# Low parts of weight tiles: from a subtraction on GpSimd to a negating copy on ScalarE and an accumulating DMA, with VectorE behind the LayerNorm

## The chip, the cores and the metric

The kernel runs on one core of a Trainium2 chip. The metric is the device time of one execution in microseconds (us); lower is better. Engines are TensorE (PE in the profile, PEld for its weight loads), VectorE (DVE), ScalarE (ACT), GpSimd (POOL) and SyncE (SP), which issues DMAs.

## The reference, cut to what matters

Two layers of a backbone are computed for 128 context tokens and 512 latent tokens, width 1024, all in float32. Each layer normalizes and modulates its input, applies one combined input projection and four branches (A convolution with LayerNorm, B long "Hyena" convolution, C pooling, D attention), gates and projects each branch, merges them and applies an output projection.

```python
def parallel_mixer(h, p, latent, k_ctx, v_ctx):
    u = h @ p['w_in']                                  # 1024 x 11264
    ...
    ya = (conformer_conv(a_glu, ...) * silu(a_gate)) @ p['wo_conv']
    yb = (hyena(b_proj, ...) * silu(b_gate)) @ p['wo_hyena']
    yc = (multiscale_pool(c_in, ...) * silu(c_gate)) @ p['wo_pool']
    yd = (att * silu(d_gate)) @ p['wo_attn']
    gm = sigmoid(g_merge).reshape(B, L, N_BRANCH, D_MODEL)
    merged = gm[:, :, 0] * ya + gm[:, :, 1] * yb + gm[:, :, 2] * yc + gm[:, :, 3] * yd
    return merged @ p['w_out'], k, v
```

## The kernel before, in words

All 640 tokens go through a layer together. A product of a weight matrix and an activation keeps float32 accuracy by splitting both into a high part (the type fp32r, which TensorE multiplies in one pass) and a low part (the remainder): each block of 128 rows costs three matmuls, high by high, high by low and low by high (`proj`, line 378). A matmul's weights are a tile of 128 partitions by up to 1024 columns: eight blocks of 128x128 for a slice of the input projection, four for the projections of the branches with 512 channels, one for the pooling matrices.

`weights` (line 331) makes such a tile. It takes a place in the ring `wr` (three places, `NHI`), SyncE loads the float32 weights into a buffer `raw` (two buffers, `NRAW`; line 340), ScalarE casts them into `whi` (line 341), and the low part `wlo` is `raw - whi`, written by GpSimd or VectorE (line 342). The flag `pooled[0]` chooses: it is false for the first three tiles of the program and during the output projection of each layer (`out_proj`, line 1758), and true otherwise. A `raw` buffer is free for its next load once `wlo` is written; `whi` and `wlo` are free once TensorE has read them.

The order of work: per layer `layers` runs the Hyena inputs, gates, values, keys and first queries; the Hyena convolutions, attention and their helpers are threads beside it. Then follow the merge of branch B, the inputs of convolution and pooling, the merge of attention (`merge`, line 796: for each of eight blocks one tile of `w_in` for the gate and one of the branch's projection), the pooling gate (`Pooling.gated`: four pairs of a `w_in` tile and a 128x128 pooling matrix), the merge of pooling, the convolution's gate, its merge and the output projection. `Conv.norm` is a thread: the LayerNorm of branch A, which ends (line 1636) while the merge of pooling runs.

TensorE's order is written out by a planner (`Loom`): it keeps a clock per engine from rough costs, runs the thread that could start first by priority, and counts the work of `weights` as background that only advances the clock of its engine. The other engines' orders are set by a scheduler from priorities, with `weights` moved ahead by `WAHEAD` (120). Every engine runs its own list in order, and SyncE's DMAs wait in order too. Instructions of VectorE, ScalarE and GpSimd carry the line of a helper, 179, matmuls 194, transposes 203.

Of the kernel before, what the change touches and what calls it, by code (L numbers as in the profile page):

```python
# [12 lines left out]
AF = mybir.ActivationFunctionType  # L13
ALU = mybir.AluOpType
# [52 lines left out]
def r32(ap):  # L67
    return ap.bitcast(F32)
# [165 lines left out]
def hybrid_flow_backbone(ctx: ExitStack, tc: tile.TileContext, i, o):  # L234
    nc = tc.nc
    lm = Loom()
    pe = Tensor(lm, nc.tensor)
    dve = Engine(lm, nc.vector, "dve", 1.0, 75)
    act = Engine(lm, nc.scalar, "act", 0.84, 130)
    pool = Engine(lm, nc.gpsimd, "pool", 2.1, 150)  # L240
# [19 lines left out]
    def nm(p):  # L260
        count[0] += 1
        return f"{p}{count[0]}"
# [65 lines left out]
        lm.dma = max(lm.dma, lm.issue + 1.2) + int(np.prod(dst.shape)) * 4 / 360e3  # L328
        return lm.dma + 1.9

    def weights(src, kk, n, pl=False):
        yield from wr.get()
        lm.bg = True
        with tc.high_priority(offset=WAHEAD):
            raw = wp.tile([P, 1024], F32, tag="raw", name=nm("raw"), bufs=NRAW)
            hi = wp.tile([P, 1024], F32R, tag="whi", name=nm("whi"), bufs=NHI)
            lo = wp.tile([P, 1024], F32R, tag="wlo", name=nm("wlo"), bufs=NHI)
            w = kk * n
            rv = raw[:, 0:w]
            sp.dma_start(out=rv.rearrange("p (k c) -> p k c", k=kk), in_=src)  # L340
            act.copy(hi[:, 0:w], rv)
            (pool if pooled[0] or pl else dve).tensor_tensor(out=lo[:, 0:w], in0=rv, in1=r32(hi[:, 0:w]), op=ALU.subtract)
        lm.bg = False
        return (hi[:, 0:w].rearrange("p (k c) -> p k c", k=kk),
                lo[:, 0:w].rearrange("p (k c) -> p k c", k=kk))

    def w_cols(l, c0):
        return weights(i["w_in"][l][:, c0:c0 + 128].rearrange("(k p) c -> p k c", p=P), 8, 128)
# [447 lines left out]
    def merge(l, b, ga, nk, wo, merged, mode, ma=None, wait=None):  # L796


        for d in range(8):
            th = yield from tr.get(T)  # L800

            def gate(j, ps):
                act.activation(out=th[:, 320 * j:320 * j + 320], in_=ps, func=AF.Tanh, scale=0.5)

            yield from in_proj(l, C_GM + b * D + 128 * d, gate)
            if wait is not None:
                yield wait
            w = yield from weights(wo[:, 128 * d:128 * d + 128].rearrange("(k p) c -> p k c", p=P), nk, 128)
            def take(j, ps):
                tj = th[:, 320 * j:320 * j + 320]  # L810
                dve.scalar_tensor_tensor(out=tj, in0=tj, scalar=1.0, in1=ps, op0=ALU.add, op1=ALU.mult)

            yield from both(w, 0, ga, nk, take)
            wr.put(WD)
            if mode == "first":
                sp.dma_start(out=mscr[l, d], in_=th)
                lm.cur.t += 2.5
            else:
                yield lambda: 0.0 if len(merged) == 2 else INF
                mv = merged[d // 4].v((d % 4) * T, T)  # L820
                dve.tensor_tensor(out=mv, in0=mv, in1=th, op=ALU.add)
                if mode == "last":
                    split(ma.h(d), ma.l(d), mv, 0.5)
            tr.put()

    hT = [None]
    pooled = [False]
# [691 lines left out]
    class Conv:  # L1519
# [58 lines left out]
        def norm(self):  # L1578
# [55 lines left out]
            sc.put()  # L1634
            co.free()
            self.ev_norm.set()

        def gated(self):
            l = self.l
# [425 lines left out]
```

## Time and profile before

| what | value |
|---|---|
| median of 3 runs (lowest, highest) | 2356.2 us (2354.53, 2362.07) |
| the profiled execution: its own time, its span | 2361.16 us, 2359.4 us |
| mean granted clock of TensorE | 0.977 |
| busy: TensorE, VectorE, ScalarE, GpSimd | 94%, 66%, 41%, 32% of the span |
| DMA, mean over the span | 80 GB/s |

The profile is of one execution, 5.0 us above the median of the runs. A stage is a stretch of the span: the first layer's Hyena stage lies at 60 to 340 us, its attention at 340 to 790, its dense projections up to 1190; the second layer has them at 1240 to 1560, 1560 to 1900 and up to the end. In a row of the trace the text `out<-in` gives tiles: `whi`, `wlo`, `raw` are the weights, `mm`, `ax`, `sc` are banks of PSUM, `sl`, `t`, `u`, `k`, `wx`, `nb` are work tiles in SBUF.

### The profile page before, as it was taken

The numbers are of one execution on the slowest core, as the hardware profiler recorded it, in microseconds if no ns is written. First come the engines' busy times: TensorE is split into PE (matmuls) and PEld (weight loads), VectorE is DVE, ScalarE is ACT, GpSimd is POOL, SyncE is SP. The second block draws the span as 40 slices with busy tenths as digits, with TensorE's granted clock in tenths as the row PEclk, the third lists the DMA queues.
The fourth block names the chain that finished last, engine by engine and source line by source line (L and its number), as shares of the span: only waits on it lengthen the run. The fifth ranks groups of instructions, "written<-read, shape, count | busy, mean of one in ns | idle before, by whom it ended". The sixth has DMA issues, their size and how long they took to land.

```text
span 2359.4 us, 39530 instructions
## 1 busy us (share of the span) xinstructions
PE 2216.7 (94%) x15951; PEld 2161.7 (92%) x15951; DVE 1558.2 (66%) x2962; ACT 960.2 (41%) x1900; POOL 747.1 (32%) x423
## 2 busy tenths in 40 slices
PE   5999989999999999999979888899999999999999
PEld 3988878999999999999969888899989999999999
DVE  4887897577558997133477787956675599842343
ACT  4533335555554224222354332455556532332231
POOL 1745432112222333333056353221212233333320
PEclk8999999999999999999989998999999999999999
DMA  8333321112112322233532211111111132222332
GB/s 266 103 106 95 107 74 54 60 57 62 46 45 77 98 62 83 77 94 90 167 120 57 58 48 45 48 58 61 57 51 49 43 115 72 59 86 72 99 98 85
DMA packets 284804, 189.10 MB, mean 80 GB/s; under 512 B 8445, under 2 KB 275901, under 8 KB 284366
## 3 DMA queue, kind: packets, MB, share of 16 engines
q1 hardware_dynamic: 284622, 186.59, 26.1%
q8 instruction: 125, 2.05, 0.4%
q14 instruction: 57, 0.47, 0.1%
HBM read 174.34 MB, written 12.22 MB: 79 GB/s over the span
## 4 chain that ended last, share of the span: by engine, by line
PE 56%; DVE 17%; ACT 2%; issue 1%; POOL 1%; DMA 0%; ACTq 0%; POOLq 0%; DVEq 0%; SPq 0%
PE mm L194 46%; DVE sl L179 6%; PE sc L194 4%; PE ax L194 3%; PE ax L203 3%; DVE u L179 2%; DVE sc L179 2%; DVE nb L179 1%; DVE k L179 1%; DVE wx L179 1%; DVE h L179 1%; ACT u L179 1%; DVE t L179 1%; DVE rt L179 1%; POOL sl L179 1%
## 5 line engine op out<-in xcount | busy, mean ns | idle before, releaser
L194 PE MATMUL mm<-sl,whi 128*128 128x320 f32 x6304 | 1420.2, 313 | 7.8 <-DVE t L179 5.0
L194 PEld LDWEIGHTS mm<-sl,whi 128*128 128x128 f32 x6304 | 1054.9, 189 | 15.5 <-DVE t L179 4.0
L194 PE MATMUL mm<-sl,wlo 128*128 128x320 f32 x3152 | 979.9, 311 | 0.9 <-DVE wlo L179 0.9
L179 POOL TENSOR_TENSOR wlo<-raw,whi 128x1024 fp32r<-128x1024 f32 (+2 forms) x253 | 550.0, 2174 | 1209.5 <-ACT whi L179 1122.9
L194 PEld LDWEIGHTS mm<-sl,wlo 128*128 128x128 f32 x3152 | 596.0, 189 | 1.2 <-DVE wlo L179 1.2
L179 ACT CAST whi<-raw 128x1024 fp32r<-128x1024 f32 (+2 forms) x272 | 255.3, 939 | 521.6 <-PE mm L194 371.3
L194 PE MATMUL mm<-whi,sl 128*128 128x256 f32 x1600 | 295.0, 286 | 0.3 <-ACT t L179 0.3
L179 DVE SCALAR_TENSOR_TENSOR t<-t,mm 128x320 f32<-128x320 f32 x192 | 92.8, 484 | 269.0 <-PE mm L194 212.2
L194 PE MATMUL sc<-sl,sl 128*128 128x128 f32 (+1 forms) x1344 | 219.3, 309 | 48.7 <-DVE sl L179 26.1
L194 PEld LDWEIGHTS mm<-whi,sl 128*128 128x128 f32 x1600 | 248.2, 190 | 2.3 <-issue 1.2
L194 PEld LDWEIGHTS sc<-sl,sl 128*128 128x128 f32 x1344 | 190.2, 206 | 55.7 <-issue 25.5
L194 PE MATMUL mm<-wlo,sl 128*128 128x256 f32 x800 | 226.0, 282 | 0.0
L179 DVE SCALAR_TENSOR_TENSOR sc<-sl,prm,sc 128x640 f32<-128x640 f32 (+14 forms) x232 | 207.0, 892 | 7.4 <-ACT sc L179 2.5
L179 DVE TENSOR_TENSOR h<-ax,h 128x512 fp32r<-128x512 f32 (+1 forms) x200 | 117.4, 602 | 137.9 <-ACT h L179 137.4
L179 ACT ACTIVATE u<-sc,nb,rq 128x640 f32<-128x640 f32 x128 | 113.4, 886 | 111.4 <-DVE nb L179 88.8
L194 PEld LDWEIGHTS mm<-wlo,sl 128*128 128x128 f32 x800 | 152.3, 190 | 0.2 <-POOL wlo L179 0.2
L179 ACT ACTIVATE t<-mm 128x320 f32<-128x320 f32 x208 | 90.1, 434 | 144.1 <-PE mm L194 143.6
L203 PE MATMUL ax<-ident,u 128*128 128x128 f32 x752 | 117.2, 277 | 15.2 <-DVE sl L179 12.0
L179 ACT CAST h<-ax 128x512 fp32r<-128x512 f32 (+1 forms) x200 | 99.9, 519 | 71.8 <-PE ax L203 70.5
L194 PE MATMUL ax<-h,sl 128*128 128x256 f32 (+1 forms) x656 | 120.0, 295 | 1.2 <-DVE h L179 0.8
L179 DVE TENSOR_REDUCE nb<-sc 128x1 f32<-128x640 f32 x128 | 104.9, 819 | 19.7 <-PE sc L194 19.0
L203 PEld LDWEIGHTS ax<-ident,u 128*128 128x128 f32 x752 | 93.1, 142 | 21.7 <-issue 12.4
(193 smaller groups left out, 2246.7 us busy)
## 6 DMA issues: line engine op xcount, KB each, us to landing
raw<-in_w_in_dram SPq DMA_DIRECT2D x176, 512.0 KB
wlo<-in_w_ada_dram SPq DMA_DIRECT2D x19, 512.0 KB
whi<-in_w_ada_dram SPq DMA_DIRECT2D x19, 512.0 KB
raw<-in_wo_attn_dram SPq DMA_DIRECT2D x16, 512.0 KB
raw<-in_w_out_dram SPq DMA_DIRECT2D x16, 512.0 KB
sl<-in_c_decay_dram SPq DMA_DIRECT2D x16, 320.0 KB
mscr<-t SPq DMA_DIRECT2D x16, 320.0 KB
sl<-mscr SPq DMA_DIRECT2D x4, 1280.0 KB
```

The costliest lines, as they stand in the source:

```text
L179: r = f(*args, **kw)
L194: r = self.real.matmul(out, lhsT, rhs, **kw)
L203: r = self.real.transpose(out, in_, ident)
```

## The change

Where `pooled[0]` is true, the low part is now made in two steps: ScalarE writes `-whi` into `wlo`, and a DMA issued by GpSimd adds `raw` to it. Where it is false, VectorE subtracts, as before. `pooled[0]` is set to false at the end of `Conv.norm` in each layer (it is set to true again as before). The unused argument `pl` goes. GpSimd's other work stays.

```diff
-    def weights(src, kk, n, pl=False):
+    def weights(src, kk, n):
...
             act.copy(hi[:, 0:w], rv)
-            (pool if pooled[0] or pl else dve).tensor_tensor(out=lo[:, 0:w], in0=rv, in1=r32(hi[:, 0:w]), op=ALU.subtract)
+            if pooled[0]:
+
+                act.activation(out=lo[:, 0:w], in_=r32(hi[:, 0:w]), func=AF.Copy, scale=-1.0)
+                nc.gpsimd.dma_start(out=r32(lo[:, 0:w]), in_=rv, accum_op=ALU.add)
+            else:
+                dve.tensor_tensor(out=lo[:, 0:w], in0=rv, in1=r32(hi[:, 0:w]), op=ALU.subtract)
...
             sc.put()
             co.free()
             self.ev_norm.set()
+            pooled[0] = False
```

Over the program, 253 subtractions on GpSimd become 187 pairs of a copy on ScalarE and a DMA on GpSimd's queue (157 of 1024 columns, 22 of 512, 8 of 128), and 66 more subtractions on VectorE (32 of 1024 columns, 34 of 512), which had 19. The engines' orders move at these places. Names: a number stands for one buffer's use, and differs between the two programs.

GpSimd's list in the second layer's Hyena convolutions, before (`sl` of 640 and `wx` of 128 columns are products and sums of the spectra):

```order
L179 TENSOR_TENSOR sl_14152<-sl_12677,sl_13773 128x640
L179 TENSOR_TENSOR wx_12037<-sl_12677 128x128 x2
L179 TENSOR_TENSOR wlo_14896<-raw_14894,whi_14895 128x1024
L179 TENSOR_TENSOR sl_13780<-sl_12677,sl_12824 128x640
L179 TENSOR_TENSOR wx_12037<-sl_12677 128x128 x2
L179 TENSOR_TENSOR wlo_15040<-raw_15038,whi_15039 128x1024
```

and the same place after the change:

```order
L179 TENSOR_TENSOR sl_14256<-sl_12740,sl_13874 128x640
L345 DMA wlo_14937<-raw_14935 128x1024
L179 TENSOR_TENSOR wx_12129<-sl_12740 128x128 x2
L179 TENSOR_TENSOR sl_13881<-sl_12740,sl_12936 128x640
L345 DMA wlo_15007<-raw_15005 128x1024
L179 TENSOR_TENSOR wx_12129<-sl_12740 128x128 x2
```

The DMA takes the subtraction's place in the list, one product earlier or later.

ScalarE's list in the first layer's pooling gate after the change, from the cast of one `w_in` tile to the copy of the next (`sl<-t` is the high part of a gated pooling output, `t<-mm` a gate):

```order
L179 CAST whi_9511<-raw_9510 128x1024
L179 CAST sl_9412<-sl_7636 128x512
L179 ACTIVATE wlo_9512<-whi_9511 128x1024
L179 CAST sl_9412<-sl_7636 128x128
L179 CAST sl_9412<-sl_7636 128x512
L179 ACTIVATE t_9416<-mm_9424 128x320
L179 CAST whi_9576<-raw_9575 128x128
L179 ACTIVATE t_9416<-mm_9457 128x320
L179 ACTIVATE wlo_9577<-whi_9576 128x128
L179 CAST whi_9596<-raw_9595 128x1024
L179 ACTIVATE sl_9412<-t_9416 128x640
L179 ACTIVATE wlo_9597<-whi_9596 128x1024
```

The rows `wlo<-whi` are new; the last of them stands behind a copy that waits for VectorE.

VectorE's list in the merge of pooling, behind the LayerNorm, after the change:

```order
L179 TENSOR_TENSOR wlo_10425<-raw_10423,whi_10424 128x1024
L179 TENSOR_TENSOR wlo_10483<-raw_10481,whi_10482 128x512
L179 SCALAR_TENSOR_TENSOR t_10328<-t_10328,mm_10393 128x320
L179 SCALAR_TENSOR_TENSOR t_10328<-t_10328,mm_10407 128x320
L179 TENSOR_TENSOR sl_8374<-sl_8374,t_10328 128x640
```

The two subtractions are new; the other three rows, which gate one block and add it to the merged sum, followed each other directly before.

## Rows read from the trace of the kernel before

**Rows 1.** The page's busy time, share of the span and instructions, by engine.

```profile
PE 2216.7 (94%) x15951; PEld 2161.7 (92%) x15951; DVE 1558.2 (66%) x2962; ACT 960.2 (41%) x1900; POOL 747.1 (32%) x423
```

**Rows 2.** Windows by stage: length, busy us per engine (instructions), clock, DMA share, GB/s.

```profile
60.00:340.00 280.00, 258.32 (x2012) 245.78 (x2013) 233.13 (x415) 110.38 (x218) 142.11 (x93) 0.98 0.33 100
340.00:790.00 450.00, 427.28 (x3080) 418.66 (x3080) 313.54 (x727) 235.75 (x498) 99.28 (x45) 0.99 0.20 60
1240.00:1560.00 320.00, 280.74 (x2014) 277.37 (x2014) 257.06 (x520) 119.81 (x243) 130.14 (x81) 0.92 0.17 51
1560.00:1900.00 340.00, 329.71 (x2397) 323.62 (x2396) 209.28 (x487) 189.68 (x399) 71.06 (x32) 0.99 0.19 57
```

**Rows 3.** Groups by form: GpSimd, 1240 to 1560 us; ScalarE, whole run: busy us, mean ns.

```profile
L179 POOL TENSOR_TENSOR wlo<-raw,whi 128x1024 fp32r<-128x1024 f32 x25 | 64.3, 2573 | 69.2 <-ACT whi L179 69.2
...
L179 ACT CAST whi<-raw 128x1024 fp32r<-128x1024 f32 x208 | 218.2, 1049 | 377.8 <-PE mm L194 234.5 <-issue 118.7 <-PE ax L194 9.5
```

**Rows 4.** Groups by form on VectorE, 1240 to 1560 us: busy us, mean ns.

```profile
L179 DVE TENSOR_TENSOR sl<-wx 128x512 f32<-128x512 f32 x44 | 45.3, 1067 | 1.0
L179 DVE SCALAR_TENSOR_TENSOR sl<-t,prm,sl 128x641 f32<-128x641 f32 x24 | 33.7, 1408 | 12.3 <-ACT sl L179 12.1
L179 DVE TENSOR_TENSOR wx<-sl,sl 128x640 f32<-128x640 f32 x8 | 11.4, 1425 | 0.2
```

**Rows 5.** The tile wx on VectorE, whole run: duration ns min/median/max.

```profile
L179 DVE TENSOR_TENSOR sl<-wx x96: 674/684/2900, 64.2 to 1478.4; 128x512 f32<-128x512 f32 x96
L179 DVE TENSOR_TENSOR sl<-sl,wx x16: 810/812/819, 119.0 to 1472.7; 128x640 f32<-128x640 f32 x16
```

**Rows 6.** Chain of waits, 1240 to 1560 us: shares by engine, tile and line.

```profile
by line: DVE sl L179 25.5%; PE mm L194 19.3%; PE sc L194 13.0%; DVE wx L179 8.1%; PE ax L194 4.3%; DVE k L179 4.3%; POOL sl L179 4.1%; issue 3.5%; DVE rt L179 3.0%; PE ax L203 2.3%; POOL wlo L179 1.5%; DVE kv L179 1.3%; DVE qv L179 1.1%; DV
```

**Rows 7.** The tile nb on VectorE: whole run (min/median/max); 340 to 790 us (mean).

```profile
L179 DVE TENSOR_TENSOR nb<-nb,rq x128: 142/158/1941, 369.6 to 1883.0; 128x1 f32<-128x1 f32 x128
...
L179 DVE TENSOR_TENSOR nb<-nb,rq 128x1 f32<-128x1 f32 x64 | 20.0, 313 | 1.2
```

**Rows 8.** Waits of TensorE, whole run: us in total, times, longest.

```profile
PE sc L194 <- ACT u L179: 11.9, 11, 2.1
```

**Rows 9.** The page's DMA queues: packets, MB, share of 16 engines.

```profile
q1 hardware_dynamic: 284622, 186.59, 26.1%
```

**Rows 10.** Timeline, steady part of attention's output projection: start us, us, instruction.

```profile
823.77 0.37 SPq L340 DMA_DIRECT2D raw<-in_wo_attn_dram  x1
...
837.69 0.37 SPq L340 DMA_DIRECT2D raw<-in_wo_attn_dram  x1
...
835.26 2.40 POOL L179 TENSOR_TENSOR wlo<-raw,whi 128x1024 fp32r<-128x1024 f32 x1 [4.67 <-ACT whi L179]
...
848.38 0.31 PE L194 MATMUL mm<-sl,wlo 128*128 128x320 f32 x1
```

**Rows 11.** Timeline, pooling gate of the first layer, by engine.

```profile
887.19 0.37 SPq L340 DMA_DIRECT2D raw<-in_w_in_dram  x1
...
894.91 0.37 SPq L340 DMA_DIRECT2D raw<-in_w_in_dram  x1
...
903.29 0.37 SPq L340 DMA_DIRECT2D raw<-in_w_in_dram  x1
...
912.33 0.37 SPq L340 DMA_DIRECT2D raw<-in_w_in_dram  x1
...
922.68 0.37 SPq L340 DMA_DIRECT2D raw<-in_w_in_dram  x1
...
891.36 1.05 ACT L179 CAST whi<-raw 128x1024 fp32r<-128x1024 f32 x1 [0.35 <-PE mm L194]
...
892.49 2.40 POOL L179 TENSOR_TENSOR wlo<-raw,whi 128x1024 fp32r<-128x1024 f32 x1 [1.28 <-ACT whi L179]
...
901.02 0.31 PE L194 MATMUL mm<-sl,wlo 128*128 128x320 f32 x1
```

**Rows 12.** Groups by form on VectorE, 945 to 1190 us.

```profile
L179 DVE TENSOR_TENSOR wlo<-raw,whi 128x1024 fp32r<-128x1024 f32 x8 | 9.8, 1222 | 21.3 <-ACT whi L179 21.2
```

## The prediction

> **What bounds the kernel now.** Read the busy line first: TensorE is busy 94% of the span, so an edit on other engines can win only the time in which TensorE stands still, and can lose whatever it makes TensorE wait for [rows 1]. The table by stage says where it stands still: 21.7 us in the first layer's Hyena stage (280.00 less 258.32), 22.7 us in its attention, 39.3 us in the second layer's Hyena stage, 10.3 us in its attention [rows 2]. In the stage from 1240 us the granted clock is also 0.92, so part of that stretch ran at 1.2 instead of 2.4 GHz. Outside these four stages TensorE loses little but the start and the change of layer.
>
> The chain of waits in the second Hyena stage says who is late there: VectorE's rows add up to 43.3% of it (25.5, 8.1, 4.3, 3.0, 1.3 and 1.1), GpSimd's subtractions of weights to 1.5% [rows 6]. VectorE is slow there because GpSimd works beside it. An addition of 128x512 from two SBUF operands takes 684 ns in the median of its 96 cases, but 2900 at worst, and 1067 in the mean of this stage; a two-operand pass over 640 columns takes 812 ns where nothing disturbs it [rows 5], while the 641-column short convolution takes 1408 and the spectrum product 1425 here [rows 4]. GpSimd's subtraction for a full weight tile is 2573 ns long there, 25 times [rows 3].
>
> The dense stages (attention's output, pooling, convolution and output projections) are the opposite: TensorE never waits, and the question is how far ahead the weights are. In the steady part loads into one raw buffer go out at 823.77 and 837.69, 13.9 us apart for two tiles, the second as soon as GpSimd is done with that buffer at 835.26 + 2.40 = 837.66; TensorE reads that low part at 848.38, so it is 10.7 us ahead [rows 10]. In the pooling gate, where each pair of tiles is one of 7 us and one of under 1 us of TensorE, the lead has shrunk to 901.02 − (892.49 + 2.40) = 6.1 us, and loads go out 7.72, 8.38, 9.04 and 10.35 us apart [rows 11].
>
> **The change part by part.** *Removed:* 253 subtractions on GpSimd, the full ones some 2.5 us each [rows 3]. *Added:* 187 negating copies on ScalarE (157 of 1024 columns, 22 of 512, 8 of 128) and 187 accumulating DMAs, issued by GpSimd, from the raw tile into the low tile. *Moved:* 66 subtractions to VectorE, 32 full and 34 half, all behind the LayerNorm.
>
> The 66 on VectorE cost 1.22 us a full tile [rows 12], about 32 × 1.22 + 34 × 0.7 = 63 us, in stages where TensorE is saturated and they end sooner than GpSimd's 2.5 us would. VectorE's idle time hides them; I count them as 0. If that cover were gone, the lead of the weights on TensorE would have to be used up first.
>
> *ScalarE.* A copy of 1024 columns takes 1.05 us [rows 3], so 157 + 11 + 1 full ones are 177 us more on an engine that has 960 [rows 1], 18%. TensorE waits for ScalarE's exponentials 11.9 us in all [rows 8]; 18% of that is 2 us, and for its other users I take 4 us in total (bounds 0 and 15, by every wait for an exponential more than doubled).
>
> *Relief of VectorE.* In the second Hyena stage three groups lose 44 × (1067 − 684) = 16.9, 24 × (1408 − 812) = 14.3 and 8 × (1425 − 812) = 4.9 us, 36 us together [rows 4, 5]. Weight tiles are about half of GpSimd's work there (64.3 of 130.14 us [rows 2, 3]), and 43% of the chain is VectorE's. From below that is 36 × 0.5 × 0.43 = 8 us; from above it is the whole pause, 39 us. I take 20, since GpSimd's own queue shortens too. For the first layer's Hyena stage I take 10 of its 21.7 us, by the same half. In attention the small product nb on the chain of scores takes 313 ns in the mean where its median is 158: 64 × 155 ns = 9.9 us in one layer [rows 7]; I take 7 for both layers. Gains: 37 us; from below 8, from above the four pauses, 94.
>
> *The price of the DMA.* No row shows an accumulating DMA. Call X the time from the end of the negating copy to the low part being usable and the raw buffer being free. A load of 512 KB takes at most 891.36 − 887.19 = 4.17 us from issue to use [rows 11]. The queue moved 186.59 MB in 26.1% of sixteen engines' span [rows 9], or 303 KB per us, so 524 KB are 1.73 us of it and 2.44 us are fixed. Bounds for X: 2.4 us if only the fixed part counts, 10 if issuing by software doubles it and three passes (read, read, write) follow each other. One pass gives 4.2, two passes 5.9. I take 5.0, between them, because rows here are 4 KB in SBUF instead of the 512-byte pieces of a weight column block.
>
> The Trainium skill (DMA: Bandwidth & Descriptors, Anatomy of one DMA) puts a DMA issued by GpSimd at 2.0 us plus its bytes at 436 GB/s, and the page Collectives: The Full Stack (on ReduceScatter) gives an adding transfer half the rate because of its second read. Estimated from these two, X is 2.0 + 2.4 = 4.4 us and the sum below would be 7 us better; no run so far shows either.
>
> *What X costs.* In the dense stages the raw buffers set the pace, since there are two: load, cast, negate, accumulate, load again. That takes 4.17 + 1.05 + 0.1 + 1.05 + X = 6.4 + X, and at X = 5 it is 11.4 us. In the steady part two full tiles come every 13.9 us, so nothing is lost, and the lead of 10.7 us falls by X + 1.05 − 2.4 = 3.65 to about 7. In the pooling gate 11.4 stands against 7.72, 8.38, 9.04 and 10.35: short by 3.7, 3.0, 2.35 and 1.05, with the first 3.65 makes 13.7, less the lead of 6.1: some 8 us of waiting per layer, 16 in all. As a rule for two layers: 2 × (5X − 17.4) us, nothing below X = 3.5. SP's queue holds its later loads back behind each raw load that waits; in the second Hyena stage 25 tiles come in 320 us, 12.8 us apart, so nothing hangs on that at this X.
>
> *Sum against the profiled execution, 2361.2 us:* −20 − 10 − 7 + 4 + 16 = −17, so 2344. The median of the runs shown lies 5.0 us below that execution; the forecast is 2339 us.
>
> **The rivals.** *The accumulation is slow and the weights become the bound.* If X is 8 us, the cycle is 14.4 us; the pooling gate is short by 6.7 + 6.0 + 5.4 + 4.05 + 6.65 − 6.1 = 23 us, with the pair behind it about 28 per layer, 56 in all, less 33 of net gain: +23, 2379 us. Against the forecast's 16 the gain is used up at X = 6.8. For it speaks that the transfer reads two streams through the engines that carry the loads; against it that they are 26.1% busy [rows 9]. Chance 0.27.
>
> *The relief doesn't reach TensorE.* Every Hyena step has also transforms on TensorE and GpSimd's own products in its chain [rows 6], and the planner writes TensorE's order anew from other cost clocks. With gains of 20 instead of 37 it ends at 2356. Chance 0.13.
>
> *VectorE holds the issue back.* GpSimd's and VectorE's two-operand work stretch each other in this trace (684 to 2900 ns [rows 5]). If writing the descriptors is held off in the same way, X grows by up to one VectorE pass, 0.8 us, and the sum by 8: 2347. Chance 0.08, half of it within 0.3%. The Trainium skill (SBUF — State Buffer, two separate sides) states such a lock for descriptors issued by GpSimd, under VectorE's two-port modes; whether it holds here no run shows yet.
>
> *GpSimd isn't freed.* If issuing takes GpSimd about as long as the subtraction did and blocks VectorE alike, the edit doesn't do what its words say: gains near 0, 20 us of cost, 2376. Chance 0.04.
>
> **How the numbers follow.** The forecast has 0.48. A measurement of this kernel can tell about 0.3%, 7 us, from no change. Faster by more than that: the forecast and half of the third rival, 0.52. Within it: the second rival and the other half, 0.17. Slower: the first and the last rival, 0.31. The range goes from 2308 (gains of 55 at X below 3.5) to 2400 (X about 9), which leaves out the slowest transfers and the largest relief; by itself the forecast would have 2315 to 2349.
>
> **What would show it.** Right: GpSimd's busy time falls from 747 us to below 400; the 128x512 addition's mean falls towards 700 ns in the stage from 1240 us, and that stage and the first Hyena stage get shorter together by some 30 us; a raw tile's next load goes out 5 us after its negating copy ends; TensorE's waits for the low part appear in the pooling gate alone. Wrong: waits of TensorE for low parts in the steady dense part (X over 7), Hyena stages of unchanged length with VectorE's passes at their clean durations (the bound lies elsewhere), or waits for ScalarE that grow by more than 15 us.

## The result, and the profile after

The changed kernel takes 2324.0 us in the median of 4 runs (2320.96 to 2330.75), the kernel before on the same chip 2355.4 (2352.56 to 2362.07): ratio 0.9859, 95% interval 0.9838 to 0.988, faster by 1.4%. The forecast was 2339 us with the change's sign and its mechanism; the gain is nearly twice the forecast's. The sum was made between profiled executions; there the change is from 2361.2 to 2324.2 us, 37 us, where the sum had 17.

The page's busy line after the change, to be laid beside [rows 1]:

```profile
PE 2209.2 (95%) x15951; PEld 2159.5 (93%) x15951; DVE 1428.7 (62%) x3028; ACT 1118.4 (48%) x2087; POOL 355.2 (15%) x357
```

GpSimd fell from 747.1 to 355.2 us, ScalarE rose by 158.2 us, and VectorE, which took over 66 subtractions, fell by 129.5 us all the same.

Where the time went is best read in stretches of equal work, not of equal time: TensorE has 15951 matmuls in both programs, so a stretch is cut where the same number of them has run. The columns are the length, then busy us (instructions) of TensorE, its weight loads, VectorE, ScalarE and GpSimd, then clock, DMA share and GB/s. The seven stretches are the first Hyena stage, its attention, the pooling gate with the merge behind it, the other dense projections, and for the second layer the Hyena stage, attention and pooling gate. The Hyena stretches end later than the stages of [rows 2] (at 400 and 1580 us instead of 340 and 1560), and the threads of a layer run beside each other, so the line between the Hyena stage and attention isn't sharp. The kernel before:

```profile
60.38:400.11 339.73, 308.79 (x2369) 293.70 (x2370) 284.81 (x589) 141.24 (x289) 153.27 (x100) 0.97 0.30 91
400.11:860.09 459.98, 446.90 (x3202) 440.82 (x3201) 327.96 (x632) 220.44 (x448) 115.13 (x51) 1.00 0.22 64
860.09:1000.13 140.04, 139.13 (x943) 138.05 (x942) 75.95 (x116) 44.62 (x76) 50.39 (x27) 1.00 0.25 74
1000.13:1240.16 240.03, 227.39 (x1666) 221.50 (x1665) 112.74 (x177) 92.27 (x191) 79.13 (x53) 0.97 0.38 117
1240.16:1580.06 339.90, 300.64 (x2159) 297.17 (x2159) 266.58 (x540) 130.78 (x265) 135.20 (x84) 0.93 0.18 53
1580.06:2030.06 450.00, 439.54 (x3135) 433.28 (x3134) 325.85 (x629) 211.31 (x426) 113.22 (x51) 0.99 0.21 63
2030.06:2140.12 110.06, 105.81 (x714) 104.27 (x713) 57.81 (x93) 37.37 (x65) 40.28 (x22) 1.00 0.25 72
```

and after the change:

```profile
59.98:378.55 318.57, 302.34 (x2368) 290.51 (x2369) 236.41 (x585) 163.61 (x313) 108.28 (x100) 0.98 0.55 139
378.55:835.93 457.38, 446.37 (x3202) 441.91 (x3201) 298.08 (x627) 264.91 (x501) 42.93 (x49) 0.99 0.50 117
835.93:989.69 153.76, 143.35 (x943) 141.04 (x942) 84.26 (x134) 56.31 (x93) 17.04 (x18) 0.98 0.46 108
989.69:1225.62 235.93, 226.20 (x1666) 221.03 (x1665) 116.01 (x199) 92.76 (x189) 31.76 (x30) 0.98 0.41 122
1225.62:1538.01 312.39, 294.35 (x2160) 291.58 (x2159) 210.94 (x536) 156.10 (x296) 87.82 (x84) 0.96 0.46 107
1538.01:1984.42 446.41, 437.69 (x3136) 433.23 (x3134) 298.93 (x620) 255.81 (x478) 43.62 (x49) 0.99 0.50 117
1984.42:2103.05 118.63, 109.64 (x715) 107.18 (x714) 68.32 (x114) 46.87 (x80) 14.47 (x16) 0.97 0.49 112
```

The lengths differ by -21.2, -2.6, +13.7, -4.1, -27.5, -3.6 and +8.6 us, -36.7 in all: the whole change of the profiled executions. The two Hyena stages gain 48.7, attention 6.2, and the two pooling gates lose 22.3. In the Hyena stages VectorE's busy time falls by 48.4 and 55.6 us for nearly the same instructions (589 and 585, 540 and 536). Its rows in the second Hyena stage (busy us, mean ns), after, to be laid beside [rows 4]:

```profile
L179 DVE TENSOR_TENSOR sl<-wx 128x512 f32<-128x512 f32 x44 | 28.3, 685 | 0.8
L179 DVE SCALAR_TENSOR_TENSOR sl<-t,prm,sl 128x641 f32<-128x641 f32 x24 | 22.7, 945 | 16.4 <-ACT sl L179 16.2
...
L179 DVE TENSOR_TENSOR wx<-sl,sl 128x640 f32<-128x640 f32 x8 | 7.1, 886 | 0.6
...
L179 DVE TENSOR_TENSOR wx<-sl 128x256 f32<-128x256 f32 x8 | 4.4, 547 | 0.0
...
L179 DVE TENSOR_TENSOR sl<-sl,sl 128x128 f32<-128x128 f32 x4 | 1.1, 279 | 0.0
```

and two forms that [rows 4] don't have, before:

```profile
L179 DVE TENSOR_TENSOR wx<-sl 128x256 f32<-128x256 f32 x8 | 9.0, 1126 | 0.0
...
L179 DVE TENSOR_TENSOR sl<-sl,sl 128x128 f32<-128x128 f32 x4 | 4.1, 1016 | 0.0
```

The 128x512 addition is back at its clean 685 ns, from 1067. TensorE's own busy time for the same matmuls fell too, 308.79 to 302.34 and 300.64 to 294.35, at a granted clock of 0.98 and 0.96 instead of 0.97 and 0.93.

The pooling gate of the first layer and the merge behind it show the price of the DMA. The timeline of the merge's first full tiles (start us, us, engine, instruction), to be laid beside [rows 11]:

```profile
889.49 0.37 SPq L340 DMA_DIRECT2D raw<-in_w_in_dram  x1
...
893.65 1.05 ACT L179 CAST whi<-raw 128x1024 fp32r<-128x1024 f32 x1 [5.62 <-DMA raw<-in_w_in_dram]
...
894.93 1.05 ACT L179 ACTIVATE wlo<-whi 128x1024 fp32r<-128x1024 f32 x1
...
896.27 0.86 POOL L345 DMA_DIRECT2D wlo<-raw  x1 [9.22 <-ACT wlo L179]
...
901.49 0.62 PE L194 MATMUL mm<-sl,wlo 128*128 128x320 f32 x1 [2.70 <-DMA wlo<-raw]
901.50 0.37 SPq L340 DMA_DIRECT2D raw<-in_w_in_dram  x1
...
906.90 1.05 ACT L179 ACTIVATE wlo<-whi 128x1024 fp32r<-128x1024 f32 x1
...
912.84 0.37 SPq L340 DMA_DIRECT2D raw<-in_w_in_dram  x1
```

The negating copy ends at 894.93 + 1.05 = 895.98, GpSimd issues at 896.27, the low part is read at 901.49 and the raw buffer loaded again at 901.50: X is 5.5 us, and the cycle from load to load 12.0 us (forecast 5.0 and 11.4). This is the longest case: the next full tile has 912.84 - (906.90 + 1.05) = 4.9 us and a cycle of 11.3, and of the 17 full tiles that are accumulated in the two gate stretches 13 have an X of 4.9 us, the others 5.0 to 5.5. TensorE waits for some of them; its waits for low parts in the whole run, its wait for ScalarE in the first gate stretch (us, times, longest) and the page's DMA rows (KB each, median us from issue to landing; the queue's packets, MB and share) are:

```profile
PE mm L194 <- DMA wlo<-raw: 18.8, 11, 3.5
...
PE mm L194 <- ACT t L179: 2.7, 1, 2.7
```

```profile
q0 software_dynamic: 26928, 88.62, 20.7%
...
wlo<-raw POOLq DMA_DIRECT2D x157, 512.0 KB, 4.7
...
wlo<-raw POOLq DMA_DIRECT2D x22, 256.0 KB, 3.5
```

Of the 18.8 us, 9.3 are in the two gate stretches; 8.6 are in the two attention stretches and 0.8 in the first Hyena stretch, where the forecast had none. The 22.3 us of the gates are those 9.3, one wait in each of 2.7 and 2.8 us until ScalarE has read a gate from its bank (`t<-mm`, which stands in its list behind passes of the LayerNorm; before the change TensorE didn't wait there), and 8 us of longer matmuls (139.13 to 143.35 and 105.81 to 109.64, the clock at 0.98 and 0.97 instead of 1.00); TensorE's other waits there fell by 0.7 us.

### The profile page after: what moved, and what is told of

It is laid out like the page before. It is cut to its first block, busy times and chain, and to the rows that moved or that the text cites. A ratio compares the mean times of both kernels' runs of the same rounds, so it can differ in the third digit from the quotient of the medians.

```text
span 2322.4 us, 39948 instructions
## 1 busy us (share of the span) xinstructions
PE 2209.2 (95%) x15951; PEld 2159.5 (93%) x15951; DVE 1428.7 (62%) x3028; ACT 1118.4 (48%) x2087; POOL 355.2 (15%) x357
## 4 chain that ended last, share of the span: by engine, by line
PE 74%; DVE 10%; DMA 8%; ACT 4%; issue 3%; POOL 1%; SPq 1%; POOLq 0%; ACTq 0%; DVEq 0%
PE mm L194 58%; PE ax L194 6%; PE sc L194 5%; DVE sl L179 5%; PE ax L203 4%; DMA wlo<-raw 3%; DMA raw<-in_w_in_dram 2%; DVE wx L179 1%; ACT u L179 1%; DVE k L179 1%; POOL sl L179 1%; DMA sl<-in_hy_w_dram 1%; DMA whi<-in_w_ada_dram 1%; SPq L326 1%; DVE u L179 1%
## 5 line engine op out<-in xcount | busy, mean ns | idle before, releaser
L345 POOL DMA_DIRECT2D wlo<-raw x187 | 161.7, 865 | 1194.4 <-ACT wlo L179 759.9
L194 PE MATMUL sc<-sl,sl 128*128 128x128 f32 (+1 forms) x1344 | 208.4, 298 | 9.4 <-DVE sl L179 5.7
L179 DVE TENSOR_TENSOR wlo<-raw,whi 128x1024 fp32r<-128x1024 f32 (+1 forms) x85 | 86.8, 1021 | 188.4 <-ACT whi L179 188.1
L194 PEld LDWEIGHTS sc<-sl,sl 128*128 128x128 f32 x1344 | 182.8, 198 | 13.1 <-issue 5.5
L179 ACT ACTIVATE wlo<-whi 128x1024 fp32r<-128x1024 f32 (+2 forms) x187 | 182.4, 975 | 1.6
L179 ACT ACTIVATE t<-mm 128x320 f32<-128x320 f32 x208 | 90.1, 434 | 114.6 <-PE mm L194 114.2
```

The lines of the kernel that those rows point to most:

```text
L179: r = f(*args, **kw)
L194: r = self.real.matmul(out, lhsT, rhs, **kw)
L345: nc.gpsimd.dma_start(out=r32(lo[:, 0:w]), in_=rv, accum_op=ALU.add)
```

## The experiments

All ratios are to the kernel before, run on the same chips; its medians were 2355.4 to 2359.8 us. Where an experiment says that TensorE's order is kept, the list of its instructions is the same from first to last.

**1. Is it the path, or the planner's new order?** The change alters two things at once: who makes the low part, and, through the planner's charges, the order written out for TensorE. First the old path in the new order.

```diff
-                act.activation(out=lo[:, 0:w], in_=r32(hi[:, 0:w]), func=AF.Copy, scale=-1.0)
-                nc.gpsimd.dma_start(out=r32(lo[:, 0:w]), in_=rv, accum_op=ALU.add)
+                lm.element("act", (w * 0.84 + 130) / 1e3)
+                nc.gpsimd.tensor_tensor(out=lo[:, 0:w], in0=rv, in1=r32(hi[:, 0:w]), op=ALU.subtract)
```

> The change's program with one thing put back: where the accumulating path stood, GpSimd subtracts again, while the planner is charged as in the change, so TensorE's order is the change's, instruction for instruction. Contention theory (GpSimd's subtractions stretch VectorE's two-operand passes, and the Hyena stages wait for VectorE): the Hyena stages are as long as before within 10 us, VectorE's 128x512 addition has a mean of about 1000 ns in the second Hyena stage, the pooling gate loses nothing, 2340 to 2360 us. Order theory (TensorE's new order made the gain): the some 53 us of the Hyena stages stay and the price of the DMA goes, about 2300 us.

Measured: 2408.0 us, ratio 1.0201 (1.0187 to 1.0216), 49 us slower than before. The order did not make the gain, but both expectations missed: with GpSimd subtracting, the change's order is a bad one. The part behind the LayerNorm was then run alone:

```diff
             self.ev_norm.set()
+            pooled[0] = False
```

> The kernel before with the moved part alone: VectorE subtracts behind the end of the LayerNorm, GpSimd elsewhere. My theory: TensorE is saturated there, no change beyond 3 us, 2352 to 2359 us. Rival (the part behind the LayerNorm carries a share of the gain): 2345 us or less.

Measured: 2359.8 us, ratio 1.0002 (0.9993 to 1.0011). That part is worth nothing, as forecast, and its TensorE order is that of the kernel before. The fourth corner, the new path in the old order:

```diff
-                act.activation(out=lo[:, 0:w], in_=r32(hi[:, 0:w]), func=AF.Copy, scale=-1.0)
+                lm.element("pool", (w * 2.1 + 150) / 1e3)
+                nc.scalar.activation(out=lo[:, 0:w], in_=r32(hi[:, 0:w]), func=AF.Copy, scale=-1.0)
                 nc.gpsimd.dma_start(out=r32(lo[:, 0:w]), in_=rv, accum_op=ALU.add)
```

> The fourth corner of the square: the change's path for the low parts, but with the planner charged as if GpSimd still subtracted, so TensorE's order is, instruction for instruction, that of the kernel before with the LayerNorm part alone (2360 us). The other corners: GpSimd's subtraction with that order 2360, with the change's order 2408; the change's path with its own order 2324. If the path alone makes the gain, 2310 to 2335 us with this order too. If path and order gain only together (the order has to know what is free), 2345 us or more.

Measured: 2297.3 us, ratio 0.9744 (0.9727 to 0.9761). The path alone gains 61 us (2358.2 to 2297.3); the order that came with it takes 27 us back. The seven stretches of equal work:

```profile
61.35:378.85 317.50, 304.44 (x2369) 292.94 (x2369) 239.44 (x590) 164.24 (x316) 107.46 (x99) 0.97 0.55 139
378.85:824.56 445.71, 442.50 (x3202) 439.16 (x3201) 304.05 (x635) 264.94 (x497) 45.49 (x51) 1.00 0.51 121
824.56:971.07 146.51, 142.14 (x943) 139.60 (x942) 75.70 (x124) 53.76 (x90) 13.68 (x15) 0.99 0.45 109
971.07:1208.04 236.97, 227.83 (x1666) 221.77 (x1665) 116.39 (x201) 94.41 (x193) 30.35 (x29) 0.97 0.40 120
1208.04:1511.63 303.59, 289.07 (x2158) 286.57 (x2158) 218.45 (x539) 156.63 (x296) 87.26 (x84) 0.98 0.47 107
1511.63:1963.72 452.09, 441.24 (x3135) 434.96 (x3134) 308.07 (x632) 254.65 (x474) 44.63 (x50) 0.99 0.51 117
1963.72:2075.81 112.09, 108.18 (x714) 105.85 (x713) 56.79 (x101) 45.13 (x77) 11.13 (x12) 0.98 0.45 107
```

Against the change the first layer's attention and pooling gate are 11.7 and 7.3 us shorter, the second layer's Hyena stage and pooling gate 8.8 and 6.5 (457.38, 153.76, 312.39 and 118.63 there), with nearly the same DMAs (181 instead of 187); the second layer's attention is 5.7 us longer, and the other two differ by 1 us. Against the kernel before, and so with TensorE's order held, the Hyena stages gain 22.2 and 36.3 us, attention gains 14.3 and loses 2.1, and the price in the two gates is 6.5 + 2.0 = 8.5 us, not 22.3.

**2. VectorE's stretching, or GpSimd's full queue?** Taking the weights off GpSimd does two things: its two-operand passes no longer run beside VectorE's, and its queue is free for its own products of spectra. To part them, VectorE makes all the low parts (with a TensorE order of that kernel's own, which the runs built on it keep), so that nothing waits for GpSimd's weight work, and a pass that nobody reads is put back on GpSimd.

```diff
-            if pooled[0]:
-
-                act.activation(out=lo[:, 0:w], in_=r32(hi[:, 0:w]), func=AF.Copy, scale=-1.0)
-                nc.gpsimd.dma_start(out=r32(lo[:, 0:w]), in_=rv, accum_op=ALU.add)
-            else:
-                dve.tensor_tensor(out=lo[:, 0:w], in0=rv, in1=r32(hi[:, 0:w]), op=ALU.subtract)
+            dve.tensor_tensor(out=lo[:, 0:w], in0=rv, in1=r32(hi[:, 0:w]), op=ALU.subtract)
```

> Every low part is subtracted by VectorE, 1.2 us a full tile: no subtraction on GpSimd and no accumulating DMA anywhere. Contention theory: VectorE gets about 25 x 1.2 = 30 us of work in each Hyena stage in place of some 59 us of stretching, and the price of the DMA (some 22 us in the two pooling gates) goes: 2300 to 2330 us. Rival (VectorE's own work is the bound, and each microsecond put on it in the Hyena stages ends in the time): 2345 us or more.

Measured: 2299.3 us, ratio 0.9745 (0.9731 to 0.9759): faster than the change, with no DMA at all. Then with the pass of two operands, or that of one, behind this line:

```diff
+            if pooled[0]:
+                nc.gpsimd.tensor_tensor(out=rv, in0=rv, in1=r32(hi[:, 0:w]), op=ALU.subtract)
```

> The kernel in which VectorE makes every low part, with a pass put on GpSimd for each tile where the flag is true: once VectorE is done with the raw tile, GpSimd subtracts the high part from it in place (two SBUF operands, about 2.5 us); nobody reads that result, and TensorE's order is unchanged. TensorE can wait for it through GpSimd's queue and the raw buffers alone. Contention theory: VectorE's passes are stretched as before, and most of the some 54 us of the two Hyena stages go again, 2340 to 2370 us. Queue theory: about the same time as the one-operand pass of the next run, within 8 us.

```diff
+            if pooled[0]:
+                nc.gpsimd.tensor_scalar(out=rv, in0=rv, scalar1=-1.0, scalar2=None, op0=ALU.mult)
```

> The same with a pass of one operand: GpSimd multiplies the raw tile by -1 in place, about 2.65 us, so its queue is as full as in the run before this one. Contention theory: VectorE's 128x512 addition stays near 700 ns and the time within 15 us of the kernel without the pass, 2298 to 2315 us. Queue theory (GpSimd's own products come late behind the passes): 2335 us or more in both runs. In between, both count, and the two differences give their shares.

Measured: two operands 2449.9 us, ratio 1.0387 (1.0369 to 1.0405); one operand 2346.3 us, ratio 0.9938 (0.9926 to 0.9951). The two Hyena stages without a pass, with the one-operand pass, and with the two-operand pass, and GpSimd's rows for the pass (busy us, mean ns):

```profile
59.83:377.73 317.90, 301.60 (x2369) 290.00 (x2369) 266.13 (x606) 138.05 (x282) 87.37 (x72) 0.98 0.33 100
...
1210.16:1520.83 310.67, 291.28 (x2160) 288.29 (x2158) 246.37 (x563) 129.62 (x262) 67.08 (x53) 0.97 0.20 60
```

```profile
58.66:390.73 332.07, 305.39 (x2369) 291.61 (x2370) 276.31 (x606) 138.14 (x282) 164.31 (x100) 0.97 0.31 94
...
1233.93:1554.93 321.00, 292.42 (x2160) 288.89 (x2159) 258.59 (x563) 129.00 (x262) 151.50 (x84) 0.97 0.20 60
```

```profile
L344 POOL TENSOR_SCALAR raw<-raw 128x1024 f32<-128x1024 f32 x167 | 488.0, 2923 | 853.6 <-DVE wlo L179 602.2 <-issue 94.0 <-DVE nb L179 44.9
```

```profile
60.45:422.88 362.43, 315.00 (x2368) 298.49 (x2369) 313.93 (x606) 138.74 (x282) 153.75 (x100) 0.95 0.29 87
...
1291.77:1637.02 345.25, 297.58 (x2158) 291.28 (x2158) 293.95 (x562) 127.88 (x260) 143.87 (x84) 0.95 0.18 55
```

```profile
L344 POOL TENSOR_TENSOR raw<-raw,whi 128x1024 f32<-128x1024 f32 x167 | 422.4, 2530 | 947.6 <-DVE wlo L179 643.8 <-issue 142.9 <-DVE nb L179 47.3
```

The one-operand pass is the longer of the two (2923 against 2530 ns), so GpSimd's queue is at least as full with it. It costs the Hyena stages 14.2 and 10.3 us; the second operand adds 30.4 and 24.3 us, while VectorE's busy time for the same instructions goes from 276.31 to 313.93 and from 258.59 to 293.95. So some 70% of the effect (54.6 of 79.1 us) is the stretching, and the rest the queue, the longer hold of the raw buffer and the little that one operand stretches. Both theories count; the one-operand pass ended 47 us over the kernel without it, where the contention theory had at most 15. The two passes differ in their operation as well, and only the second reads `whi`; no run parts these from the number of operands.

**3. The negating copy on GpSimd.** The same question within the change:

```diff
-                act.activation(out=lo[:, 0:w], in_=r32(hi[:, 0:w]), func=AF.Copy, scale=-1.0)
+                lm.element("act", (w * 0.84 + 130) / 1e3)
+                nc.gpsimd.tensor_scalar(out=lo[:, 0:w], in0=r32(hi[:, 0:w]), scalar1=-1.0, scalar2=None, op0=ALU.mult)
```

> The change with the negating copy moved from ScalarE to GpSimd: GpSimd works one pass per tile again, but with one SBUF operand in place of two, and the order of TensorE is the change's. Contention theory: a pass with one operand does not stretch VectorE, so the Hyena stages keep most of their gain, 2315 to 2335 us. Queue theory (it is GpSimd's own products of spectra that came earlier once its queue was empty): its queue is filled again, and half of the some 53 us of the Hyena stages or more go, 2345 to 2370 us.

Measured: 2406.5 us, ratio 1.0195 (1.0179 to 1.0211), outside both. The pass and TensorE's wait for what comes behind it:

```profile
L345 POOL TENSOR_SCALAR wlo<-whi 128x1024 fp32r<-128x1024 f32 (+2 forms) x187 | 495.6, 2650 | 810.5 <-ACT whi L179 810.2
```

```profile
PE mm L194 <- DMA wlo<-raw: 44.5, 21, 5.2
```

The low part now comes late: 2.65 us of GpSimd, then the DMA, and TensorE waits 44.5 us for it instead of 18.8. This run mixes the queue with the lateness of the weights and so decides nothing between the two theories; the pair above does.

**4. The price of the DMA and ScalarE's share.** VectorE from the pooling gate on, then the accumulating path left on through the merges:

```diff
+            pooled[0] = False
             yield from po.gated()
```

> The change, with VectorE taking the low parts from the start of the pooling gate on, not from the end of the LayerNorm. If the price of the accumulating DMA lies in the pooling gate and the merge behind it (13.8 and 8.5 us by the two traces), this takes some 22 us off the change: 2297 to 2306 us. If the gate is slow for another reason (VectorE's LayerNorm, ScalarE), 2318 us or more.

```diff
             self.ev_norm.set()
-            pooled[0] = False
```

> The change without its last line: the accumulating path goes on behind the LayerNorm, up to the output projection. By the raw-buffer rule (a full tile holds its buffer 6.4 us plus 4.7 us of DMA = 11.1 us, while TensorE takes a full and a half tile in 10.5 us), about 0.6 us is lost in each of some 18 pairs per layer, 20 us more than the change: 2335 to 2355 us. If the buffers are not the limit, 2320 to 2328 us, as the change.

Measured: 2300.0 us, ratio 0.9749 (0.9736 to 0.9763), and 2364.3 us, ratio 1.0019 (1.001 to 1.0027). The first takes 24 us off the change, as expected, and its two gate stretches are 23.2 us shorter: the price lies in the gate. Its TensorE order differs from the change's from matmul 6172 on, within the first gate stretch, so this doesn't say how much of that price is the DMA's; with the order held, in experiment 5, the same move takes 10.6 us. The second costs 40 us more than the change, above the expected 11 to 31. SP's loads in the steady merge of the convolution tell why:

```profile
1034.22 0.37 SPq L340 DMA_DIRECT2D raw<-in_w_in_dram  x1
...
1045.88 0.37 SPq L340 DMA_DIRECT2D raw<-in_w_in_dram  x1
...
1058.32 0.37 SPq L340 DMA_DIRECT2D raw<-in_w_in_dram  x1
```

Loads of full tiles go out 11.66 and 12.44 us apart, so the cycle is about 12 us, not 11.1, against 10.5 us of TensorE: 1.5 us a pair where 0.6 was expected, and TensorE's waits for low parts are 43.8 us in the whole run instead of 18.8. Over all pairs that would be more than 40 us; that the lead of the weights covers the first ones was not traced.

ScalarE's copies alone, on the kernel in which VectorE makes every low part:

```diff
+            if pooled[0]:
+                nc.scalar.activation(out=rv, in_=rv, func=AF.Copy, scale=-1.0)
```

> The kernel in which VectorE makes every low part, with a copy on ScalarE for each tile where the flag is true: once VectorE is done with the raw tile, ScalarE multiplies it by -1 in place, as long as the change's negating copy (about 1.05 us), and nobody reads that result; TensorE's order is unchanged. It is the forecast's ScalarE term alone, 4 us with bounds 0 and 15 (for some 207 copies instead of 187): 2299 to 2315 us, 2303 likeliest. If the copies on ScalarE carry a larger part of the change's cost, 2315 us or more.

Measured: 2301.1 us, ratio 0.9756 (0.9743 to 0.9769), 1.7 us over the kernel without them, with intervals that overlap: ScalarE's term is small.

GpSimd's own products, moved to VectorE (the six calls of the Hyena stages and of the LayerNorm, such as this one):

```diff
-            pool.tensor_tensor(out=zt, in0=x[:, :, 1], in1=h[:, :, 1], op=ALU.mult)
+            dve.tensor_tensor(out=zt, in0=x[:, :, 1], in1=h[:, :, 1], op=ALU.mult)
```

> VectorE makes every low part, and GpSimd's products and sums in the Hyena stages and the LayerNorm go to VectorE as well (only the powers stay on GpSimd), so that no two-operand pass of GpSimd of any length is left. Contention theory: what is left of the stretching, some 29 us of VectorE, goes, and GpSimd's 1.5 to 2.0 us products become 0.8 us ones in the chain; against it VectorE gets some 60 us more work. 2285 to 2305 us. If VectorE has become the bound: 2310 us or more.

Measured: 2298.2 us, ratio 0.9746 (0.9733 to 0.976): nothing to tell from the kernel without that move. The stretching is gone (the longest of the 96 additions of 128x512 takes 695 ns, against 2900 in the kernel before), and VectorE has more work; but TensorE's order is another as well, so what each of the three is worth this run doesn't tell.

**5. What makes the new order poor.** VectorE's path in the old order, and the two paths put together in it (the flag `vec` is set ahead of the pooling gate and cleared at the start of a layer):

```diff
+                lm.element("pool", (w * 2.1 + 150) / 1e3)
+                nc.vector.tensor_tensor(out=lo[:, 0:w], in0=rv, in1=r32(hi[:, 0:w]), op=ALU.subtract)
```

> VectorE makes every low part, and the planner is charged as if GpSimd did, so TensorE's order is the one of the kernel before. If the old order is worth some 27 us with any path that leaves GpSimd free, as with the accumulating one (2324 against 2297), this lands near 2272 to 2285 us. If the old order helps only because the accumulating path's lateness is covered by it (the pooling gate lost 8.5 us there instead of 22), it stays at 2290 to 2300 us, as with the planner's own order (2299).

```diff
+                lm.element("pool", (w * 2.1 + 150) / 1e3)
+                if vec[0]:
+                    nc.vector.tensor_tensor(out=lo[:, 0:w], in0=rv, in1=r32(hi[:, 0:w]), op=ALU.subtract)
+                else:
+                    nc.scalar.activation(out=lo[:, 0:w], in_=r32(hi[:, 0:w]), func=AF.Copy, scale=-1.0)
+                    nc.gpsimd.dma_start(out=r32(lo[:, 0:w]), in_=rv, accum_op=ALU.add)
```

> The accumulating path up to the pooling gate, VectorE from there on, with TensorE's order of the kernel before. Against the run with that order and the accumulating path through the gate (2297 us) the rest of the DMA's price goes, 8.5 us by its trace: 2286 to 2293 us. If the price there was none of the DMA's, 2294 to 2300 us.

Measured: 2330.6 us, ratio 0.988 (0.9864 to 0.9897), outside both expectations, and 2286.7 us, ratio 0.9694 (0.9679 to 0.9708), as expected of the DMA's price: 10.6 us under the accumulating path through the gate (2297.3), in the same order. The old order isn't better for every path: VectorE's path is 31 us slower in it than in its own. The second run is the fastest of the study. Then the planner's two charges, with the change's path in all four cases: nothing charged, or both.

```diff
-                act.activation(out=lo[:, 0:w], in_=r32(hi[:, 0:w]), func=AF.Copy, scale=-1.0)
+                nc.scalar.activation(out=lo[:, 0:w], in_=r32(hi[:, 0:w]), func=AF.Copy, scale=-1.0)
```

> The change with another charge in the planner: nothing for a tile on the accumulating path (the change charges ScalarE 0.99 us for the negating copy). If ScalarE's charge is what makes the change's order poor, this is near the old order's 2297 us, within 10. If it is the missing charge for GpSimd, it is as poor as the change or poorer, 2318 us or more.

```diff
+                lm.element("pool", (w * 2.1 + 150) / 1e3)
                 act.activation(out=lo[:, 0:w], in_=r32(hi[:, 0:w]), func=AF.Copy, scale=-1.0)
```

> The change with both charges: ScalarE's 0.99 us for the copy and GpSimd's 2.3 us of the old subtraction. If the missing charge for GpSimd is the fault, near 2297 us, within 10. If ScalarE's charge is, 2318 us or more. If both this and the run before it come out poor, no single charge is the cause, and the order is a matter of how the threads happen to fall.

Measured: 2315.2 us, ratio 0.9814 (0.98 to 0.9828), and 2329.9 us, ratio 0.9871 (0.9855 to 0.9887). In one table (us, the change's path throughout):

| charged to GpSimd per full tile | nothing to ScalarE | 0.99 us to ScalarE |
|---|---|---|
| 2.3 us | 2297.3 | 2329.9 |
| nothing | 2315.2 | 2324.0 (the change) |

ScalarE's charge makes the order worse in both rows (by 33 and 9 us); GpSimd's helps by 18 in one column, and in the other its 6 can't be told from nothing (the intervals overlap). There TensorE's order is the same with and without GpSimd's charge up to matmul 8551 of 15951, through the whole first layer. So most of it goes with ScalarE's charge, but no single charge has the effect, and which threads fall badly was not traced. That stays open.

## Why the prediction was right and wrong

The direction and the mechanism were right; the sum was not, and that it came as near as it did is partly luck. With TensorE's order held, the stretches give Hyena -58.5, attention -12.2, gates +8.5 and the other dense projections -3.1 us, -65.3 together; the new order then takes 28.6 back, which leaves -36.7. The forecast's sum of -17 had a relief that was too small and no price for the order, and these two errors work against each other. Step by step, with the change's own stretches:

- *Relief in the Hyena stages, the step that failed by size.* Forecast -10 and -20, measured -21.2 and -27.5. The working counted three forms with 36 us of stretching in the second stage, halved for GpSimd's other work, and took 20 us between 8 and 39. But VectorE's busy time there fell by 55.6 us. The three counted forms gave back 17.0, 11.0 and 4.3 us (28.3, 22.7 and 7.1 left), 32 of the 36, so halving them was wrong; and forms that were not counted had been stretched as well (the 128x128 product from 279 to 1016 ns, the 128x256 operation into wx from 547 to 1126). Of what VectorE got back, 44% and 49% reached the end (21.2 of 48.4 and 27.5 of 55.6 us), near the chain's 43% for VectorE [rows 6]: 0.43 times the two falls would have been 45 us. In the old order it was 49% and 75% (22.2 of 45.4 and 36.3 of 48.1), so the chain's share was what arrived at the least.
- *The clock* had no term. The same matmuls took 6.5 and 6.3 us less of TensorE's time in the two Hyena stages, at a higher granted clock; that is 12.7 of the 48.7 us. The row that told of it was in [rows 2], 0.92. No run moves the clock alone, so this is a part of what the relief brought and not a cause shown apart.
- *Attention*: forecast -7, measured -6.2, although VectorE lost 29.9 and 26.9 us of busy time there. The product nb did become clean (its longest is 162 ns, from 1941), but in the old order the same path gained 14.3 us in the first layer and lost 2.1 in the second, so that the number was hit is luck.
- *ScalarE*: forecast +4, the copies alone cost +1.7, not to be told from nothing; in the change's order TensorE waits 5.5 us for it in the two gates.
- *The DMA*: forecast +16, measured +22.3 (with those 5.5 us of ScalarE's in it). X was right: 4.9 us in 13 of 17 tiles and 5.5 at most, forecast 5.0. The rule 2 x (5X - 17.4) gives 14 for 4.9. What it leaves out is the order: with the order held the path costs the two gates 8.5 us in the old one and 17.4 in the change's (153.76 and 118.63 against 145.19 and 109.85, where GpSimd subtracts in that order). Why the old order bears the same X better was not traced. The estimate from the Trainium skill (DMA: Bandwidth & Descriptors, Anatomy of one DMA, with Collectives: The Full Stack) was 4.4 us; the median from issue to landing of a 512 KB tile was 4.7, close to it, and X has besides 0.3 us from the end of the copy to the issue.
- *The subtractions on VectorE behind the LayerNorm*: forecast 0, alone 1.0002. The -4.1 us of that stretch in the change lie in the start of the second layer, which it contains.
- *The order*: named in the rival "the relief doesn't reach TensorE" and given no price. It costs 27 us here. It is the largest term that the sum lacked; that the forecast still fell short shows how much too small the relief was: the path alone gains 61.
- *The range*: its lower end is added up wrongly. Gains of 55 with 4 for ScalarE and nothing for the DMA give 2305, not 2308. The short convolution's clean 812 ns was that of another form; it takes 945 after the change.

Of the rivals, slow accumulation (X of 8) is excluded by an X of 4.9 to 5.5 in the gates, and "GpSimd isn't freed" by 355.2 us and 0.86 us an issue. That VectorE holds the issue back can't be told: the landing takes 4.7 us in the median, and nothing separates a wait in it. What would show it: GpSimd below 400, the addition near 700 ns, the next load 5 us behind the copy came as written; the Hyena stages got 49 us shorter, not 30; waits for the low part lay in the gate for half only.

The mechanism is shown by the pair of passes: in the same place, with a result that nobody reads and the same order of TensorE, the two-operand pass costs 103.5 us more than the longer one-operand pass (2449.85 less 2346.34).

## What to carry to other kernels

Price a relief from all the rows that the removed work stretches, each against its clean duration, and take the engine's share of the critical chain as the least that arrives (43% here, where 44 to 75% did). Where a planner writes an order from costs, a change of path is two changes: run the new path in the old order as well, since here the order hid 27 of 61 us. The version to keep is the accumulating path up to the pooling gate with VectorE from there on, in the old order: 2286.7 us, 3.1% under the kernel before.

## What the runs showed of the hardware that was not expected

How much a GpSimd pass stretches VectorE differs with its SBUF operands. 207 passes of two operands add 1805.1 - 1623.2 = 181.9 us to VectorE's busy time, 0.88 us each; 207 passes of one operand, though longer, add 1661.8 - 1623.2 = 38.6 us, 0.19 us each (the busy lines of the three runs):

```profile
PE 2195.1 (96%) x15951; PEld 2141.9 (93%) x15951; DVE 1623.2 (71%) x3215; ACT 959.0 (42%) x1900; POOL 205.7 (9%) x170
```

```profile
PE 2208.2 (94%) x15951; PEld 2151.2 (92%) x15951; DVE 1661.8 (71%) x3215; ACT 958.4 (41%) x1900; POOL 741.6 (32%) x377
```

```profile
PE 2234.5 (91%) x15951; PEld 2168.4 (89%) x15951; DVE 1805.1 (74%) x3215; ACT 958.3 (39%) x1900; POOL 675.0 (28%) x377
```

The Trainium skill (SBUF — State Buffer, SBUF: two separate sides) has a VectorE pass with two SBUF inputs and a GpSimd instruction that reads SBUF exclude each other: the one that starts first holds the shared port for its whole length, and the other waits. The two-operand passes agree; the one-operand passes read SBUF as well and are longer, so they should have stretched VectorE at least as much, and by the measurement they do a fifth of it.

VectorE's passes that read one operand from PSUM are stretched by neither: the 136 of the tile h from ax over 512 columns take 90.2 us without a pass, 90.1 with the one-operand pass and 90.2 with the two-operand pass.

A pass of one operand is no cheaper on GpSimd than one of two: 2923 against 2530 ns for 128x1024. An accumulating DMA from SBUF to SBUF lands after 4.7 us for 512 KB and 3.5 us for 256 KB in the median, and holds GpSimd's queue for 0.86 us. In the two gates its raw buffer is loaded again 4.9 us behind the end of the negating copy in 13 of 17 cases.
